# A trunk of S5 and gated delta layers on one core: the gated delta preparation at fixed steps, its decay and scores by whole units, its diagonal blocks inverted four chunks at a time

## The chip, the cores and the metric

The kernel runs on one core of one Trainium2 chip. The metric is device time in microseconds (us) of one execution, as the median of several runs. The core has five engines that work side by side and wait for each other through semaphores: TensorE (PE: matmuls into PSUM, its weight loads shown as PEld), VectorE (DVE), ScalarE (ACT), GpSimd (POOL) and SyncE (SP, which here only issues DMAs). Every engine works off its own program in order.

## The reference

Two layers are computed on 1,024 tokens of width 1,024. The first mixes tokens by an S5 scan; the second, where the change is, by a gated DeltaNet with 12 value heads and 6 key heads of width 128:

```python
q, k, v = jnp.split(silu(causal_conv(qkv, conv_w)), ...)     # q, k: 6 heads, l2-normed; v: 12 heads
g = -exp(a_log) * softplus(a + dt_bias);  beta = sigmoid(b)
# in chunks, with g summed up within a chunk:
decay = exp(where(causal, g[..., :, None] - g[..., None, :], -inf))
l_mat = where(strict, einsum('nbhid,nbhjd->nbhij', k * beta, k) * decay, 0.0)
t_mat = triangular_solve(l_mat, eye, left_side=True, lower=True, unit_diagonal=True)
u = t_mat @ v_beta;  w = t_mat @ (k_beta * exp(g))
intra = where(causal, (q @ k.T) * decay, 0.0)
# then a scan over the chunks with state, u, w, intra; rmsnorm; times silu(gate)
```

Each layer also attends to 256 memory tokens (4 heads), multiplies by a SiLU gate, and maps back to width 1,024.

## The kernel before, in words

The kernel uses chunks of 128 tokens, so there are 8 chunks; a chunk and a half of the heads (6 of 12) is a **unit** `(c, hf)`, 16 in all. What a chunk needs before the scan is the inverse of a unit lower triangular 128x128 matrix for each head.

**Projections.** A weight tile of 128 columns is loaded (`wraw`), split by ACT into a rounded half `whi` and by DVE into the rest `wlo`, and multiplied with the hidden state, split likewise into `hh` and `hl`. `mm3` (L110) issues three products, `pp<-hh,whi`, `pp<-hl,whi` and `pp<-hh,wlo`, for 8 slices of the width and 2 halves of the tokens: 48 matmuls of 128x512 for each tile. DVE then multiplies the two PSUM halves with the token norm (`scaled`, L260; into `cx` or `pj`). A tile is a *conv* tile (`conv`, L895: a multiplication and three multiply-adds of 128x1024 on DVE, a SiLU on ACT, then stored as `qkv`), an *attention input* or a *gate* tile (both only scaled, some with a SiLU, and stored).

**Up to the units.** `layer2` runs conv tiles 0 to 11 (q and k), turns each to token-major form by 8 transposes (`token_major`, L907: `ps_a<-ident,co`) and sums squares; `gdn_norms` (L923) makes the reciprocal norms `rq`, `rk` from them by a chain of small DVE operations, and `br` (beta times norm), which PE transposes (`ps_a<-ident,br`), ACT copies to `rows` and SP stores as `Brow`.

**A unit.** `load_kq` (L952) loads k and q; `g_scores` (L959) loads rows of G and of beta, broadcast, into `E` and `Eb`; 6 DVE operations form G_i - G_j and the causal mask (`E<-E,gG,negm`, L82), one ACT operation of 128x768 the exponential, POOL the product `Eb<-Eb,E` (L73); three matmuls `ps_a<-kq` (128x256) give k k' and k q', and 6 DVE operations multiply them out of PSUM with the norm and with `Eb` or `E` into `MT` and `AT`. The diagonal 32x32 blocks of `MT` go to DRAM (`Dm`), `AT` to `ATd`. `g_lower` (L985) transposes `MT` by 6 matmuls `ps_a<-ident,MT`; ACT copies what lies below the diagonal to `L`.

**The inverse.** `g_blocks` (L998) inverts the 32x32 diagonal blocks of one pair of chunks (96 blocks, one on each partition) by back substitution: 31 steps of two DVE operations, `XT<-XM,XN` and `XN<-XN,XT`, each over m*(32-m) elements. ACT transposes the result (`XM<-XN`), and SP stores both forms as `Dn` and `Dt`. `g_inverse` (L1017) loads the blocks of a unit (`N<-Dn`, `T<-Dt`) and builds the 128x128 inverse by four groups of small matmuls, y (`ps_a<-N,L`), z, y2 and z2, with ACT copies in between, and stores it as `Nd`.

**What sets the order.** `layer2` (L1257) runs a loop over p in 0 to 5: pair p's scores and lower parts, pair p-1's blocks, pair p-2's inverses, with three to five projection tiles (`fills`) between them. A scheduler then orders each engine's program by its own estimate of when operands are ready, so that PE takes other work where a unit's matmul isn't ready yet. Only where `self.pe.on` is set (in `before` around the S5 layer's groups) is PE kept in the order of the program: `Ordered.pin` (L44) asks for it.

After this stage come the scan steps with 8 more gate tiles, the attention, and the output projection; they are not changed.

Of the kernel before, what the change touches and what calls it, by code (L numbers as in the profile page):

```python
# [22 lines left out]
L = 1024  # L23
# [30 lines left out]
class Kern:  # L54
# [215 lines left out]
    def attention_inputs(self, h, wq, wg, rhs, wp):  # L270

        def one(w, dst, fn):
            t = self.tl(wp, (128, L), "pj")
            self.scaled(t, self.project([w], rhs), rhs[2], fn)
            self.dma(dst, t)

        return [partial(one, wq, self.qx[h], None), partial(one, wg, self.gx[h], AF.Silu)]
# [537 lines left out]
    def gdn_scalars(self, sp, wp, h):  # L815
# [68 lines left out]
        act.activation(eG, G, AF.Exp)  # L884
        self.rows(wp, G, self.Grow)
# [55 lines left out]
    def g_tiles(self, gp):  # L941
# [5 lines left out]
        self.Nb = [once(gp, (128, 6, 128), "N") for _ in range(2)]  # L947
        self.T64 = [once(gp, (64, 6, 64), "T64") for _ in range(2)]
# [10 lines left out]
    def g_scores(self, c, hf, gp):  # L959
        act, pe, tt, stt = self.act, self.pe, self.tt, self.stt  # L960
# [8 lines left out]
        act.activation(E, E, AF.Exp)  # L969
# [15 lines left out]
    def g_lower(self, MT, gp):  # L985
        act, pe = self.act, self.pe

        Lm = self.tl(gp, (128, 6, 96), "L", bufs=12)
# [9 lines left out]
    def g_blocks(self, pair, gp):  # L998

        n = 96  # L1000
        M, N = self.tl(gp, (n, 32, 32), "XM", bufs=1), self.tl(gp, (n, 32, 32), "XN", bufs=1)
        flat = "c b h j i -> (c b h) (j i)"
        self.dma(M.rearrange("p j i -> p (j i)"), self.Dm[pair].rearrange(flat))
        self.pool.memset(N, 0.0)
        self.v.memset(N.rearrange("p a b -> p (a b)")[:, 0:1024:33], 1.0)
        for m in range(31, 0, -1):
            w = 32 - m
            t = self.tl(gp, (n, 256), "XT", bufs=1)[:, 0:m * w].rearrange("p (j i) -> p j i", i=w)
# [4 lines left out]
        self.act.copy(T, N.rearrange("p j i -> p i j"))  # L1013
        for dst, src in ((self.Dn, N), (self.Dt, T)):
            self.dma(dst[pair].rearrange(flat), src.rearrange("p j i -> p (j i)"))

    def g_inverse(self, c, hf, gp, Lm):  # L1017

        act, pe = self.act, self.pe
        N, T64 = self.Nb[hf], self.T64[hf]  # L1020
# [8 lines left out]
        self.dma(T22[64:96], self.Dt[c // 2][c % 2, 2, h6].rearrange("h i j -> i h j"))  # L1029
        y = self.pa.tile([128, 6, 32], F32, name="ps_a", tag="ps_a")  # L1030
# [5 lines left out]
        for a in (0, 64):  # L1036
            act.copy(Y1[a:a + 32], y[a:a + 32])
        z = self.pa.tile([128, 6, 32], F32, name="ps_a", tag="ps_a")
# [9 lines left out]
        act.mul(T64[32:64, :, 0:32], z[32:64], -1.0)  # L1048
        y2 = self.pa.tile([128, 6, 64], F32, name="ps_a", tag="ps_a")
# [4 lines left out]
        act.copy(Y2, y2[0:64])  # L1054
        z2 = self.pa.tile([128, 6, 64], F32, name="ps_a", tag="ps_a")
# [201 lines left out]
    def layer2(self, st, h):  # L1257
# [7 lines left out]
        with P(name="cv", bufs=2, side="right") as wp:  # L1265
# [10 lines left out]
            with P(name="g1", bufs=2, side="right") as gp:  # L1276
                self.g_tiles(gp)
                units = [[(c, hf) for c in (2 * p, 2 * p + 1) for hf in range(2)] for p in range(4)]
                fills = [[partial(self.conv, ct, h, wp) for ct in range(12 + 3 * p, 15 + 3 * p)] for p in range(4)]
                fills += [[], []]  # L1280
                for hd in range(4):
                    fills[hd + 1] += self.attention_inputs(hd, A["g_w_in"][36 + hd], A["g_w_in"][40 + hd], h, wp)
                fills[4] += [partial(self.gate_tile, g, h, wp) for g in range(1)]
# [186 lines left out]
```

## Time and profile before

| what | us |
|---|---|
| median of 3 runs | 1955.84 (1953.41 to 1957.94) |
| the profiled execution's own time | 1961.59 |
| its span in the trace | 1959.9 |
| PE busy in the span | 1873.6 (96%) |
| DVE busy | 1316.7 (67%) |
| ACT busy | 941.2 (48%) |
| POOL busy | 170.9 (9%) |

The stage that the change rewrites lies between about 1118 and 1500 us of the span. The profile's page gives busy times, the chain of work that ended last, groups of instructions and DMA issues; beside it the trace can be asked for a table of windows (busy time of each engine, granted TensorE clock, DMA share), for the groups of one window, for what an engine waited for, and for a timeline of single instructions. A busy PE is not PE at its peak: a matmul's record reaches over the start of the next, so what a matmul costs is read from start to start.

### The profile page before, as it was taken

The numbers are of one execution on the slowest core, as the hardware profiler recorded it, in microseconds if no ns is written. First come the engines' busy times: TensorE is split into PE (matmuls) and PEld (weight loads), VectorE is DVE, ScalarE is ACT, GpSimd is POOL, SyncE is SP. The second block draws the span as 40 slices with busy tenths as digits, with TensorE's granted clock in tenths as the row PEclk, the third lists the DMA queues.
The fourth block names the chain that finished last, engine by engine and source line by source line (L and its number), as shares of the span: only waits on it lengthen the run. The fifth ranks groups of instructions, "written<-read, shape, count | busy, mean of one in ns | idle before, by whom it ended". The sixth has DMA issues, their size and how long they took to land.

```text
span 1959.9 us, 28842 instructions
## 1 busy us (share of the span) xinstructions
PE 1873.6 (96%) x10386; PEld 1528.9 (78%) x10386; DVE 1316.7 (67%) x2675; ACT 941.2 (48%) x1937; POOL 170.9 (9%) x100
## 2 busy tenths in 40 slices
PE   6899999999999998999999999899999999799897
PEld 6788888788878886888688877677777888588686
DVE  7888897895664423564566589869712787888744
ACT  5345688775554413443334444444334654555321
POOL 3100000000202131000000021110000000300400
PEclk9999999999999998999999999989999999999998
DMA  7445556554844434554223476656445765774752
GB/s 240 144 127 137 163 172 175 154 162 144 271 144 137 161 109 143 192 167 139 78 87 98 139 235 208 187 170 203 156 120 162 235 203 177 256 236 137 230 156 86
DMA packets 254446, 325.18 MB, mean 166 GB/s; under 512 B 80864, under 2 KB 176672, under 8 KB 254304
## 3 DMA queue, kind: packets, MB, share of 16 engines
q1 hardware_dynamic: 228960, 238.40, 39.4%
q10 hardware_dynamic: 25344, 84.95, 14.2%
q8 instruction: 82, 1.34, 0.3%
q14 instruction: 60, 0.49, 0.1%
HBM read 213.20 MB, written 93.95 MB: 157 GB/s over the span
## 4 chain that ended last, share of the span: by engine, by line
PE 77%; DVE 9%; DMA 6%; ACT 4%; issue 3%; SPq 1%; POOL 1%; ACTq 0%; DVEq 0%; POOLq 0%
PE pp L48 61%; PE ps_a L48 13%; PE ps_a L51 3%; DVE wlo L73 1%; DMA kq<-qkv 1%; SPq L70 1%; ACT whi L86 1%; DMA yr<-gy 1%; DMA zr<-oTd 1%; DVE co L82 1%; DVE E L82 1%; DVE XN L73 0%; DMA E<-Grow 0%; DVE ol L73 0%; DMA R<-E 0%
## 5 line engine op out<-in xcount | busy, mean ns | idle before, releaser
L48 PE MATMUL pp<-hh,whi 128*128 128x512 f32 x1216 | 493.4, 406 | 0.8 <-ACT hh L215 0.8
L48 PE MATMUL pp<-hl,whi 128*128 128x512 f32 x1216 | 481.9, 396 | 2.4 <-DVE hl L82 2.4
L48 PE MATMUL pp<-hh,wlo 128*128 128x512 f32 x1216 | 482.6, 397 | 0.0
L86 ACT CAST whi<-wraw 128x1024 fp32r<-128x1024 f32 (+1 forms) x180 | 183.7, 1021 | 410.5 <-PE pp L48 369.6
L73 DVE TENSOR_TENSOR wlo<-wraw,whi 128x1024 fp32r<-128x1024 f32 (+2 forms) x180 | 215.6, 1198 | 102.1 <-ACT whi L86 101.3
L48 PEld LDWEIGHTS pp<-hh,whi 128*128 128x128 f32 x1216 | 229.9, 189 | 50.8 <-issue 5.2
L48 PEld LDWEIGHTS pp<-hh,wlo 128*128 128x128 f32 x1216 | 229.7, 189 | 47.4
L48 PEld LDWEIGHTS pp<-hl,whi 128*128 128x128 f32 x1216 | 230.1, 189 | 46.0 <-DVE hl L82 3.3
L48 PE MATMUL pp<-oh,whi 128*128 128x512 f32 (+1 forms) x528 | 209.7, 397 | 9.9 <-ACT oh L86 6.8
L48 PE MATMUL pp<-oh,wlo 128*128 128x512 f32 (+1 forms) x528 | 207.8, 394 | 3.4 <-DVE wlo L73 3.3
L48 PE MATMUL pp<-ol,whi 128*128 128x512 f32 (+1 forms) x528 | 207.8, 394 | 1.5 <-DVE ol L73 1.5
L73 DVE TENSOR_TENSOR pj<-pp,hr 128x512 f32<-128x512 f32 x104 | 69.4, 687 | 115.6 <-PE pp L48 115.6
L48 PEld LDWEIGHTS pp<-oh,whi 128*128 128x128 f32 x528 | 100.5, 191 | 32.3 <-ACT oh L86 8.3
L48 PEld LDWEIGHTS pp<-oh,wlo 128*128 128x128 f32 x528 | 100.5, 190 | 26.8 <-DVE wlo L73 4.6
L48 PEld LDWEIGHTS pp<-ol,whi 128*128 128x128 f32 x528 | 100.4, 190 | 25.2 <-DVE ol L73 4.1
L48 PE MATMUL pp<-yl,whi 128*128 128x512 f32 x288 | 114.0, 396 | 0.5 <-DVE yl L73 0.5
L48 PE MATMUL pp<-yh,wlo 128*128 128x512 f32 x288 | 114.2, 396 | 0.0
L48 PE MATMUL pp<-yh,whi 128*128 128x512 f32 x288 | 113.7, 395 | 0.0
L82 DVE SCALAR_TENSOR_TENSOR co<-cx,conv_w,co 128x1024 f32<-128x1024 f32 x72 | 96.8, 1344 | 1.1
L73 POOL TENSOR_TENSOR ye<-yh,yl 128x1024 f32<-128x1024 f32 x12 | 29.7, 2478 | 617.8 <-DVE yl L73 443.0
L73 POOL TENSOR_TENSOR zr<-zr,zg 128x512 f32<-128x512 f32 x24 | 37.6, 1584 | 433.6 <-DMA kq<-qkv 296.2
L73 DVE TENSOR_TENSOR cx<-pp,hr 128x512 f32<-128x512 f32 x48 | 32.5, 688 | 58.5 <-PE pp L48 58.4
(350 smaller groups left out, 3258.0 us busy)
## 6 DMA issues: line engine op xcount, KB each, us to landing
wraw<-in_w_out_dram ACTq DMA_DIRECT2D x64, 512.0 KB, 4.0
wraw<-in_g_w_in_dram ACTq DMA_DIRECT2D x44, 512.0 KB, 4.3
wraw<-in_s_w_in_dram ACTq DMA_DIRECT2D x32, 512.0 KB, 4.0
R<-E SPq DMA_DIRECT2D x48, 256.0 KB, 3.8
gate<-pj SPq DMA_DIRECT2D x24, 512.0 KB, 3.9
qkv<-co SPq DMA_DIRECT2D x24, 512.0 KB, 2.8
kq<-qkv SPq DMA_DIRECT2D x60, 192.0 KB, 4.2
wraw<-in_w_glu_dram ACTq DMA_DIRECT2D x24, 384.0 KB, 3.6
```

The lines of the kernel that those rows point to most:

```text
L48: return self.pin(self.eng.matmul(*a, **kw))
L51: return self.pin(self.eng.transpose(*a, **kw))
L70: self.nc.sync.dma_start(out=out, in_=in_)
L73: (eng or self.v).tensor_tensor(out=out, in0=a, in1=b, op=op)
L82: self.v.scalar_tensor_tensor(out=out, in0=a, scalar=s, in1=b, op0=op0, op1=op1)
L86: self.act.copy(hi, src)
```

## The change

`layer2` hands the whole stage to a new function `g_units`, which puts everything at **steps**. A step is 6 of a tile's matmuls (one slice of the width), since projections are now generators that stop after each slice (`project_by_k`). Eight steps run ahead; from step 0 on, `self.pe.on` keeps PE in program order. The tiles follow each other as conv 12 to 18, the 8 attention inputs and 4 gates, conv 19 to 23. Unit u has its decay (loads, mask, exponential) prepared 6 steps ahead of its scores, the scores at step 6i for the first 8 units and 62+6i for the last 8, its lower part 4 steps after that. The blocks of chunks 0 to 3 begin at step 45, four of their 31 steps for every three steps of the tiles, those of chunks 4 to 7 at step 107. The inverse of unit u has its loads at s-4 and its y, z, y2 and z2 at s, s+3, s+6 and s+9, with s = 77+6i (first 8) or 139+5i (last 8).

The decay is now one masking addition of 128x768 on DVE, six exponentials of 128x128 on ACT with -G as bias (`nG`, a new small table), and `Eb*E` on DVE in place of POOL. The scores are copied out of PSUM by ACT, scaled by `rk`, over `kq`; then two DVE operations of 128x768 form `MT` in `Eb` and `AT` in `E`, so that the page will show `Eb` and `E` where it showed `MT` and `AT`. The blocks of four chunks are inverted together: the same 62 operations for a half of the sequence, each over twice the elements (`96x2x...`), and the memset, the transposing ACT copies and the stores twice for each. There are 4 `N` and 4 `T64` buffers in place of 2, 11 of `L` in place of 12, and 3 of the pool of projection tiles in place of 2, where the conv's output now shares the tag `pj`.

```diff
@@ conv
-        ps = self.project([self.A["g_w_in"][ct]], h)
-        x, o = self.tl(wp, (128, L + 3), "cx"), self.tl(wp, (128, L), "co")
+        ps = yield from self.project_by_k([self.A["g_w_in"][ct]], h)
+        x, o = self.tl(wp, (128, L + 3), "cx", bufs=2), self.tl(wp, (128, L), "pj")
@@ g_scores, now g_decay and g_scores
+        self.tt(E, E, self.negm.unsqueeze(1).broadcast_to([128, 6, 128]), ADD)
         for h in range(6):
-            stt(E[:, h], E[:, h], self.gG[:, c, 6 * hf + h:6 * hf + h + 1], self.negm, SUB, ADD)
-        act.activation(E, E, AF.Exp)
-        tt(Eb, Eb, E, MUL, self.pool)
-        AT, MT = self.tl(gp, sh, "AT"), self.tl(gp, sh, "MT")
-        for j in range(3):
-            ps = self.pa.tile([128, 2, 128], F32, name="ps_a", tag="ps_a")
-            pe.matmul(ps, lhsT=kq[:, j, 0], rhs=kq[:, j], start=True, stop=True)
-            rk = self.rk[:, c, 3 * hf + j:3 * hf + j + 1]
-            e2 = slice(2 * j, 2 * j + 2)
-            for i, (o, e) in enumerate(((MT, Eb), (AT, E))):
-                stt(o[:, e2], ps[:, i].unsqueeze(1).broadcast_to([128, 2, 128]), rk, e[:, e2], MUL, MUL)
+            q = 6 * hf + h
+            self.act.activation(E[:, h], E[:, h], AF.Exp, bias=self.gnG[:, c, q:q + 1])
+        self.tt(Eb, Eb, E, MUL)
+        return kq, E, Eb
+
+    def g_scores(self, c, hf, gp, kq, E, Eb):
+        for js in ((0, 1), (2,)):
+            ps = self.pa.tile([128, 2, 2, 128], F32, name="ps_a", tag="ps_a")
+            for j in js:
+                self.pe.matmul(ps[:, j % 2], lhsT=kq[:, j, 0], rhs=kq[:, j], start=True, stop=True)
+            for j in js:
+                q = 3 * hf + j
+                self.act.activation(kq[:, j], ps[:, j % 2], AF.Copy, scale=self.rk[:, c, q:q + 1])
+        MT, AT = Eb, E
+        for i, t in enumerate((MT, AT)):
+            t = t.rearrange("p (j e) i -> p j e i", e=2)
+            self.tt(t, kq[:, :, i].unsqueeze(2).broadcast_to([128, 3, 2, 128]), t, MUL)
@@ g_blocks
         for m in range(31, 0, -1):
             w = 32 - m
-            self.tt(t, M[:, 0:m, m:m + 1].broadcast_to([n, m, w]),
-                    N[:, m:m + 1, m:32].broadcast_to([n, m, w]), MUL)
-            self.tt(N[:, 0:m, m:32], N[:, 0:m, m:32], t, SUB)
-        T = self.tl(gp, (n, 32, 32), "XM", bufs=1)
-        self.act.copy(T, N.rearrange("p j i -> p i j"))
-        for dst, src in ((self.Dn, N), (self.Dt, T)):
-            self.dma(dst[pair].rearrange(flat), src.rearrange("p j i -> p (j i)"))
+            self.tt(t, M[:, :, 0:m, m:m + 1].broadcast_to([n, 2, m, w]),
+                    N[:, :, m:m + 1, m:32].broadcast_to([n, 2, m, w]), MUL)
+            self.tt(N[:, :, 0:m, m:32], N[:, :, 0:m, m:32], t, SUB)
+            yield
+        T = self.tl(gp, (n, 2, 32, 32), "XM", bufs=1)
+        for q in range(2):
+            self.act.copy(T[:, q], N[:, q].rearrange("p j i -> p i j"))
+            for dst, src in ((self.Dn, N), (self.Dt, T)):
+                self.dma(dst[2 * half + q].rearrange(flat), src[:, q].rearrange("p j i -> p (j i)"))
@@ g_units (new)
+        for u in range(16):
+            i, late = u % 8, u // 8
+            s = 6 * i + 62 * late
+            put(s - 6, prepare, u)
+            put(s, scores, u)
+            put(s + 4, lower, u)
+            s = (77 + 6 * i, 139 + 5 * i)[late]
+            put(s - 4, load, u)
+            for j in range(4):
+                put(s + 3 * j, inverse, u)
+        for half, s in ((0, 45), (1, 107)):
+            for i in range(32):
+                put(s + 3 * i // 4, blocks, ("b", half))
...
+        for t in range(-8, 0):
+            for what in at.pop(t, ()):
+                what()
+            next(go)
+        self.pe.on = True
+        for t in range(0, 1 + max(at)):
+            for what in at.pop(t, ()):
+                what()
+            next(go, None)
+        drain(go)
+        self.pe.on = False
```

The first place is PE where the stage begins. Before, 60 rows of `pp` stand between the last transposes of conv 11 (`ps_a<-ident_170,co`, 8 of them) and the transpose of `br`, and 25 more between that and the first scores (`ps_a<-kq`). These are the rows around `br` before:

```order
L48 MATMUL pp<-hh_7047,whi 128x512
L48 MATMUL pp<-hl_7048,whi 128x512
L48 MATMUL pp<-hh_7047,wlo 128x512
L51 MATMUL ps_a<-ident_170,br_9715 96x128
L48 MATMUL pp<-hh_7047,whi 128x512
L48 MATMUL pp<-hl_7048,whi 128x512
L48 MATMUL pp<-hh_7047,wlo 128x512
```

And the rows around it now, of which the first ones are the end of what stands behind those transposes (`ps_a<-ident_170,pj` now), 12 rows of `pp` in all:

```order
L48 MATMUL pp<-hh_7047,wlo 128x512
L48 MATMUL pp<-hh_7047,whi 128x512
L48 MATMUL pp<-hl_7048,whi 128x512
L48 MATMUL pp<-hh_7047,wlo 128x512
L51 MATMUL ps_a<-ident_170,br_9717 96x128
L48 MATMUL ps_a<-kq 128x256 x3
L48 MATMUL pp<-hh_7047,whi 128x512
L48 MATMUL pp<-hl_7048,whi 128x512
```

The scores of unit 0 now stand right behind `br`, and `br` 12 matmuls behind the last transposes in place of 60.

The second place is DVE in the middle of a block inversion; `XT` and `XN` are its two operations in turn. Before (the first pair's, with the mask operations of a unit and a conv tile's multiply-adds between them):

```order
L82 SCALAR_TENSOR_TENSOR co<-cx,conv_w_182,co 128x1024
L73 TENSOR_TENSOR XT<-XM,XN 96x207
L82 SCALAR_TENSOR_TENSOR E<-E,gG_8514,negm_9730 128x128
L73 TENSOR_TENSOR XN<-XN,XT 96x23x9
L82 SCALAR_TENSOR_TENSOR E<-E,gG_8514,negm_9730 128x128
L73 TENSOR_TENSOR XT<-XM,XN 96x220
L82 SCALAR_TENSOR_TENSOR E<-E,gG_8514,negm_9730 128x128
L73 TENSOR_TENSOR XN<-XN,XT 96x22x10
L82 SCALAR_TENSOR_TENSOR E<-E,gG_8514,negm_9730 128x128
L73 TENSOR_TENSOR XT<-XM,XN 96x231
```

And now (the first half's, with the score products `Eb<-kq,Eb` and `E<-kq,E` of unit 8 and an attention input's scaling and weight split between them):

```order
L73 TENSOR_TENSOR XT<-XM,XN 96x462
L73 TENSOR_TENSOR Eb<-kq,Eb 128x768
L73 TENSOR_TENSOR XN<-XN,XT 96x2x21x11
L73 TENSOR_TENSOR E<-kq,E 128x768
L73 TENSOR_TENSOR XT<-XM,XN 96x480
L73 TENSOR_TENSOR pj<-pp,hr_7049 128x512 x2
L73 TENSOR_TENSOR wlo<-wraw,whi 128x1024
L73 TENSOR_TENSOR XN<-XN,XT 96x2x20x12
L73 TENSOR_TENSOR XT<-XM,XN 96x494
L73 TENSOR_TENSOR XN<-XN,XT 96x2x19x13
```

Each operation of the inversion has twice the elements, and there are half as many of them in all; six small mask operations for each unit have given way to whole-unit ones.

The third place is PE where the first inverse begins (`ps_a<-N,L` is y of unit 0). Before:

```order
L48 MATMUL pp<-hl_7048,whi 128x512
L48 MATMUL pp<-hh_7047,wlo 128x512
L48 MATMUL ps_a<-N_9735,L 32x32
L48 MATMUL pp<-hh_7047,whi 128x512
L48 MATMUL pp<-hl_7048,whi 128x512
L48 MATMUL pp<-hh_7047,wlo 128x512
L48 MATMUL pp<-hh_7047,whi 128x512
L48 MATMUL pp<-hl_7048,whi 128x512
L48 MATMUL ps_a<-N_9735,L 32x32 x11
L48 MATMUL pp<-hh_7047,wlo 128x512
```

And now:

```order
L48 MATMUL pp<-hl_7048,whi 128x512
L48 MATMUL pp<-hh_7047,wlo 128x512
L48 MATMUL ps_a<-N_9737,L 32x32 x12
L48 MATMUL pp<-hh_7047,whi 128x512
L48 MATMUL pp<-hl_7048,whi 128x512
L48 MATMUL pp<-hh_7047,wlo 128x512
L48 MATMUL pp<-hh_7047,whi 128x512
L48 MATMUL pp<-hl_7048,whi 128x512
L48 MATMUL pp<-hh_7047,wlo 128x512
```

Before, the scheduler put the 12 matmuls of y apart, with `pp` rows among them; now they stand together at their step, 77, and every later `pp` row stands behind them.

More of the change, by code (lines that the diff above doesn't have):

```diff
@@ L272, in one @@
         def one(w, dst, fn):
+            ps = yield from self.project_by_k([w], rhs)
             t = self.tl(wp, (128, L), "pj")
-            self.scaled(t, self.project([w], rhs), rhs[2], fn)
+            self.scaled(t, ps, rhs[2], fn)
             self.dma(dst, t)
-        return [partial(one, wq, self.qx[h], None), partial(one, wg, self.gx[h], AF.Silu)]
+        return [one(wq, self.qx[h], None), one(wg, self.gx[h], AF.Silu)]
     def attention(self, layer, h, half, ap, dst):
@@ L884, in gdn_scalars @@
         act.activation(eG, G, AF.Exp)
+        act.mul(P("nG"), G, -1.0)
         self.rows(wp, G, self.Grow)
@@ L946, in g_tiles @@
                                 fill=-1e30, base=0, channel_multiplier=-1)
-        self.Nb = [once(gp, (128, 6, 128), "N") for _ in range(2)]
-        self.T64 = [once(gp, (64, 6, 64), "T64") for _ in range(2)]
+        self.Nb = [once(gp, (128, 6, 128), "N") for _ in range(4)]
+        self.T64 = [once(gp, (64, 6, 64), "T64") for _ in range(4)]
         for t in self.Nb + self.T64:
@@ L1054, in g_inverse @@
         act.copy(Y2, y2[0:64])
+        yield
         z2 = self.pa.tile([128, 6, 64], F32, name="ps_a", tag="ps_a")
@@ L1059, in g_inverse, with g_units, prepare, scores @@
         self.dma(self.Nd[c, hf], N)
+    def g_units(self, h, wp, gp):
+        A = self.A
+        units = [(c, hf) for c in range(8) for hf in range(2)]
+        decay, mt, low, inv = {}, {}, {}, {}
+        def prepare(u):
+            decay[u] = self.g_decay(*units[u], gp)
+        def scores(u):
+            mt[u] = self.g_scores(*units[u], gp, *decay.pop(u))
+        def lower(u):
+            low[u] = self.g_lower(mt.pop(u), gp)
+        def blocks(i):
+            if i not in inv:
+                inv[i] = self.g_blocks(i[1], gp)
+            next(inv[i], None)
+        def load(u):
+            inv[u] = self.g_inverse(*units[u], gp, low.pop(u))
+            next(inv[u])
+        def inverse(u):
+            next(inv[u], None)
+        at = {}
+        def put(t, what, arg):
+            at.setdefault(t, []).append(partial(what, arg))
+        for u in range(16):
[11 more added lines that the diff above has]
+                put(s + 3 * i // 4, blocks, ("b", half))
+        light = [one for hd in range(4) for one in
+                 self.attention_inputs(hd, A["g_w_in"][36 + hd], A["g_w_in"][40 + hd], h, wp)]
+        light += [self.gate_by_k(g, h, wp) for g in range(4)]
+        tiles = [self.conv_by_k(ct, h, wp) for ct in range(12, 19)] + light
+        tiles += [self.conv_by_k(ct, h, wp) for ct in range(19, 24)]
+        def steps():
+            for one in tiles:
+                yield from one
+        go = steps()
+        for t in range(-8, 0):
[9 more added lines that the diff above has]
+        self.pe.on = False
@@ L1264, in layer2 @@
             self.gdn_scalars(sp, wp, h)
-        with P(name="cv", bufs=2, side="right") as wp:
+        with P(name="cv", bufs=3, side="right") as wp:
             with P(name="tm", bufs=2, side="right") as tp:
@@ L1277, in layer2 @@
                 self.g_tiles(gp)
[L1278 to L1283, printed above, removed]
-                fills[5] += [partial(self.gate_tile, g, h, wp) for g in range(1, 4)]
-                Lm = {}
-                for p in range(6):
-                    mt, lag = [], []
-                    fill = iter(fills[p])
-                    if 0 < p < 5:
-                        self.g_blocks(p - 1, gp)
-                    for i in range(5):
-                        if i < 4 and p < 4:
-                            mt.append((units[p][i], self.g_scores(*units[p][i], gp)))
-                        if i and p < 4:
-                            u, m = mt.pop(0)
-                            Lm[u] = self.g_lower(m, gp)
-                        next(fill, lambda: None)()
-                        if i < 4 and p >= 2:
-                            u = units[p - 2][i]
-                            self.g_inverse(*u, gp, Lm.pop(u))
+                self.g_units(h, wp, gp)
         g2 = ExitStack()
```

29 lines of the change are left out of this document (19 added, 10 removed).

## The prediction

> **What bounds the kernel now.** I read the table of windows over the stage that is rewritten first, to see whether PE is short of work there, then the groups of instructions of that stretch, then the timelines. Columns of the table: window and length, then busy us (instructions) of PE, PEld, DVE, ACT and POOL, the granted TensorE clock, DMA share, GB/s.
>
> ```profile
> 1160.00:1200.00 40.00, 36.41 (x165) 28.37 (x164) 35.06 (x72) 17.23 (x26) 9.56 (x4) 1.00 0.75 226
> 1200.00:1240.00 40.00, 38.30 (x176) 30.74 (x175) 38.63 (x95) 20.27 (x27) 7.14 (x3) 1.00 0.67 205
> 1240.00:1280.00 40.00, 36.80 (x279) 27.52 (x278) 35.53 (x82) 17.30 (x27) 5.60 (x2) 0.87 0.56 162
> 1280.00:1320.00 40.00, 37.65 (x288) 28.47 (x287) 24.01 (x61) 19.75 (x36) 6.43 (x4) 0.87 0.65 201
> ```
>
> PE is the bound, but DVE is close behind it: 35 to 39 of 40 us up to 1280. PE idles 3.6 + 1.7 + 3.2 + 2.4 = 10.9 us in these four windows, and in the last two the granted clock is 0.87, worth 2 x 40 x 0.13 = 10.4 us. So there are some 21 us here that a smoother order could win, and not more: the matmuls themselves are the same before and after.
>
> The groups of the stretch from 1111 to 1490 us (busy us, mean ns of one | idle before):
>
> ```profile
> L82 DVE SCALAR_TENSOR_TENSOR co<-cx,conv_w,co 128x1024 f32<-128x1024 f32 x39 | 54.4, 1395 | 0.3
> L73 DVE TENSOR_TENSOR XN<-XN,XT 96x31 f32<-96x31 f32 (+15 forms) x124 | 47.1, 380 | 2.0
> L73 DVE TENSOR_TENSOR XT<-XM,XN 96x31 f32<-96x31 f32 (+15 forms) x124 | 41.7, 336 | 8.8 <-DMA XM<-Dm 6.9
> L73 POOL TENSOR_TENSOR Eb<-Eb,E 128x768 f32<-128x768 f32 x16 | 35.7, 2232 | 187.0 <-ACT E L969 169.6 <-DMA N<-Dn 17.4
> L82 DVE SCALAR_TENSOR_TENSOR E<-E,gG,negm 128x128 f32<-128x128 f32 x96 | 32.2, 359 | 2.3 <-DMA E<-Grow 2.3
> L73 DVE TENSOR_TENSOR wlo<-wraw,whi 128x1024 fp32r<-128x1024 f32 x25 | 30.5, 1222 | 1.5 <-ACT whi L86 1.3
> ...
> L48 PE MATMUL ps_a<-Y,T 32*32 32x32 f32 (+1 forms) x506 | 25.1, 210 | 1.1 <-ACT Y L1037 1.1
> L82 DVE SCALAR_TENSOR_TENSOR MT<-ps_a,rk,Eb 128x256 f32<-128x256 f32 x48 | 22.8, 475 | 10.6 <-POOL Eb L73 10.5
> ...
> L73 DVE TENSOR_TENSOR pj<-pp,hr 128x512 f32<-128x512 f32 x24 | 16.4, 691 | 70.5 <-PE pp L48 70.5
> ```
>
> **The change part by part.** *Whole-unit decay and scores.* A unit's mask and score operations cost DVE 6 x 0.359 + 3 x 0.475 + as much for AT = 5.0 us. Now there are four operations of 128x768 (mask, Eb, MT, AT). No row has that size; between the 0.69 of 512 elements and the 1.22 of 1024 it is about 0.96 each, 3.8 a unit, although Eb comes over from POOL (2.23 there). DVE wins 1.2 x 16 = 19 us. ACT gets five more exponentials and three copies a unit; it is half idle here (17 to 20 of 40 us), so I cost that at nothing beyond its place in the chain of a unit.
>
> *Double-width blocks.* These rows are from a pair's inversion that ran alone on DVE:
>
> ```profile
> 1389.71 0.20 DVE L73 TENSOR_TENSOR XT<-XM,XN 96x31 f32<-96x31 f32 x1 [4.37 <-DMA XM<-Dm]
> 1389.95 0.21 DVE L73 TENSOR_TENSOR XN<-XN,XT 96x31 f32<-96x31 f32 x1
> ...
> 1404.24 0.42 DVE L73 TENSOR_TENSOR XT<-XM,XN 96x256 f32<-96x256 f32 x1
> 1404.69 0.42 DVE L73 TENSOR_TENSOR XN<-XN,XT 96x256 f32<-96x256 f32 x1
> ```
>
> From start to start 0.24 us at 31 elements and 0.45 at 256: 0.21 us and 0.96 ns an element. The 31 steps of m(32-m) elements sum to 5,456, so a pair takes 62 x 0.21 + 2 x 5,456 x 0.96 ns = 23.5 us and a double one 13.0 + 21.0 = 34.0. Four pairs took 94, two halves take 68. DVE wins 26 us more in sum; but each half now comes as one run of 34, and what it is wanted for stands at a fixed place on PE.
>
> *The start.* What PE, DVE and SP do there now:
>
> ```profile
> 1118.40 0.77 PE L51 MATMUL ps_a<-ident,co 128*128 128x128 f32 x5
> ...
> 1133.36 0.31 PE L51 MATMUL ps_a<-ident,br 128*96 128x128 f32 x1 [0.26 <-DVE br L73]
> ...
> 1139.00 0.40 PE L48 MATMUL pp<-hh,whi 128*128 128x512 f32 x1
> 1139.24 1.02 PE L48 MATMUL ps_a<-kq 128*128 128x256 f32 x4
> ```
>
> ```profile
> 1124.24 0.20 DVE L77 TENSOR_SCALAR nv<-ssq 128x96 f32<-128x96 f32 x1
> ...
> 1131.32 0.26 DVE L82 SCALAR_TENSOR_TENSOR qke<-qkt,qke 128x96 f32<-128x96 f32 x1
> 1131.61 0.26 DVE L73 TENSOR_TENSOR qkt<-qke 128x96 f32<-128x96 f32 x1
> ```
>
> ```profile
> 1134.00 0.33 SPq L70 DMA_DIRECT2D Brow<-rows  x1
> 1134.39 0.95 SPq L70 DMA_DIRECT2D kq<-qkv  x2
> ```
>
> A pp matmul is 0.23 us from start to start. The 60 of them after the last transposes covered 13.8 us, which the DVE chain from nv to br needed. Now 12 stand there: PE is done at 1119.4 + 2.8 = 1122.2. The chain begins at 1124.24 at the earliest; its 17 operations, free of the conv tile's between them, take 0.29 each: br at 1129.2. PE idles 7.0 us. Then come the scores of unit 0: in the trace SP issued Brow 0.64 us after br's transpose, and the kq loads behind it end their issue at 1135.34; with a landing of some 3 us the scores can begin about 4 us after br (3 to 5.9, the trace's own distance from 1133.36 to 1139.24). Then 24 pp (5.5 us) until the transposes of MT_0, which need rows of E and Eb loaded through the same queue, six exponentials and three DVE operations:
>
> ```profile
> E<-Grow SPq DMA_DIRECT2D x16, 384.0 KB, 5.1
> ...
> Dm<-MT SPq DMA_DIRECT2D x64, 24.0 KB, 2.3
> XM<-Dm SPq DMA_DIRECT2D x4, 384.0 KB, 4.1
> ...
> N<-Dn SPq DMA_DIRECT2D x64, 24.0 KB, 2.2
> ```
>
> E is issued about 2 us after br, lands 5.1 later, and mask, exponentials (6 x 0.3), Eb and MT follow: br + 12, when PE is there at br + 10.5, and DVE has the mask of unit 1 queued ahead: I take 5, from 2 to 6. Start: 7 + 4 + 5 = 16 us (9 to 19).
>
> *Units 0 to 7.* PE needs 36 pp (8.3), the scores (1.0) and transposes (0.8): 10.1 us a unit. DVE needs three quarters of a conv tile (4 x 1.395 at most, 2 x 0.69 and 1.22 for wlo: 6.1) and 3.8: 9.9 at most. No wait, by a thin margin: 0 to 3 us, taken as 0.
>
> *Half 0's blocks.* The M load waits for MT_7 (scores at step 42): copies, MT, the Dm stores (four issues and 2.3), the load's 4.1: some 13 us, so it lands near step 51. From there PE has 26 steps of 1.4 us, three scores and three lower parts: 41 us to y of unit 0 at step 77. On DVE's program between the first XT and the last XN of this half stand, beside the 34.0 us of the blocks, 14 whole-unit operations of units 8 to 12 (13.4), scaling and weight split of three attention inputs (3 x 2.6) and two multiply-adds (2.8): 58 us. Behind that comes the tail that one sees here, a pair's (chain of waits):
>
> ```profile
> 1240.98 2.15 ACT XM L1013
> 1243.14 5.11 DMA Dt<-XM
> ```
>
> The transposing copies are now two (4.3), and SP stands with its program behind the second one, since both halves' Dn and Dt are issued ahead of the first N load; then four issues (1.9) and 2.2: 9 us. 58 + 9 - 41 = 26 us in which PE stands at y with every later pp behind it. Dependent operations hide some of their fixed time when others stand between them, and M can land a step or two earlier, so I take 21 (10 to 32). Before, PE took other pp there.
>
> *Half 1's blocks.* M lands near step 114, 25 steps (35 us) ahead of step 139; three inverses lie between (25.1 / 14 = 1.8 us each for the Y,T kind alone, some 3.5 in all): 46. DVE: 34 and four light tiles, 44, and the tail: 53. That is 7; I take 4 (0 to 15), since this half has little else on DVE.
>
> *The clock.* In the windows from 1240 the clock fell although no idle time of PE in them was long, and 10.4 us went. After three or four real idles I count one stretch of half clock each, 7 us in sum (3 to 12). The Trainium skill, "TensorE: Matmul & The Clock Gate", Part 1, has it that an idle window of about 3.4 us halves the clock until about 3.4 us of sustained work: an estimate from it is 1.7 us for each of four idles, 7 us, but by it the falls in the rows above should not have come at all; the rows decide, and they allow more.
>
> *What goes.* PE's waits of before in this stage (10.9) and its clock falls (10.4): -21 us if all go, and I let all go (-12 if half of the waits only move).
>
> **Sum.** 16 + 21 + 4 + 7 - 21 = +27 us on the profiled execution's 1961.6: 1988.6. The median of the runs is 5.8 below that execution, so I forecast 1983 us. Behind 1500 us nothing changes: conv 23's output stands behind the last inverses as far as I see, beside gate tiles.
>
> **The rivals.** *A, the blocks keep up (faster).* Place: y of unit 0. The run of half 0 must end within 41 - 9 = 32 us of the M load, not 58, for PE not to wait; that needs most of the other 24 us done ahead of the load, while DVE has nothing else to do. It is the point that decides. For it: DVE was under 39 of 40 us busy and now has 19 + 26 = 45 us less to do over the stage, and it may idle ahead of the load. Against it: the order has those operations between the block operations, and an engine keeps its order. With no wait at half 1 either, 3 at half 0 and 4 for the clock, the sum is the start (9 to 16) + 3 + 0 + 4 - 21 = -5 to +2 on the median, 1951 to 1958, and lower by 3 to 6 where the small matmuls, no longer strewn among pp, cost PE less: value 1951, range 1945 to 1958.
>
> *B, a draw.* Half 0 waits 8 us, the start costs 13, the clock 4: 1955.8 + 8 + 13 + 4 + 0 - 21 = 1960, a few us either way.
>
> *C, worse.* A two-level pattern (`96x2x20x12`) pays its fixed part twice: 62 x 0.21 = 13 us more on DVE in each half, which PE pays in full at both: 1983 + 26 = 2009. No row shows such a pattern.
>
> *D, the order is not held.* If PE's program were not the one printed, the waits would be filled as before and DVE's relief alone would tell: 1956 less some half of the 21 us, 1945. The printed rows speak against it.
>
> **Chances.** Forecast 0.56, A 0.24, B 0.06, C 0.08, D 0.06. The forecast's own range takes its bounds (start 9 to 19, half 0 10 to 32, half 1 0 to 15, clock 3 to 12), not all at one end: 1962 to 2003. The range reaches down to the lower end of A: 1945 to 2003. A measurement here tells about 0.2% (4 us) from no change. Faster: three quarters of A, D, little of B, 0.25; same: the rest of A and some of B, 0.08; slower: the forecast, C and the rest, 0.67.
>
> **What would show it.** In the profile of the changed kernel: PE idle of 7 us ahead of br's transpose and about 4 ahead of the first scores; one wait of PE of 10 to 30 us at the first `ps_a<-N,L`, released by a load of N, while DVE is busy without a gap from the first XT to the last XN; a small one at unit 8's; granted clock under 1 right after each. XT and XN groups of 62 with means near 0.5 us. Wrong: no wait over 5 us at the first y, or a DVE that has gaps between block operations; or a start without idle.

## The result, and the profile after

The changed kernel takes 1977.91 us (median of 4 runs, 1974.73 to 1980.69), the kernel before 1956.4 in the runs beside it: a ratio of 1.0111, with a 95% interval of 1.0091 to 1.0131. The change makes it 21.5 us slower; 27 were forecast. The profiled execution of the changed kernel took 1974.73 us, 3.2 below its median, where that of before was above its own; so the two traces are compared stage by stage and not by their ends. They differ ahead of the stage too: the last transposes of conv 11 begin at 1118.40 us in the trace before and at 1113.12 in the one after, though nothing there was changed. One of the eight runs of experiment 12 below took 2618.88 us at a granted clock of 0.65 and is left out of that kernel's median.

The table of windows of the changed kernel (columns as before):

```profile
1160.00:1200.00 40.00, 39.49 (x184) 32.58 (x182) 32.29 (x37) 30.02 (x61) 0.00 (x0) 1.00 0.85 255
1200.00:1240.00 40.00, 37.65 (x173) 31.41 (x174) 35.90 (x53) 21.45 (x42) 0.00 (x0) 1.00 0.56 181
1240.00:1280.00 40.00, 20.98 (x99) 17.19 (x97) 34.13 (x56) 19.61 (x39) 0.00 (x0) 0.82 0.60 182
1280.00:1320.00 40.00, 34.90 (x349) 28.28 (x350) 11.15 (x15) 19.71 (x47) 1.81 (x1) 0.88 0.64 177
```

The third row is the result in one line: PE is busy for 21 of 40 us while DVE works for 34. Afterwards DVE has little to do (11 of 40). DVE's load over the stage did fall; it is bunched where PE can't go on without it.

What PE waited for in the stage (1105 to 1530 us): sum, times, longest.

```profile
PE ps_a L48 <- DMA N<-Dn: 29.7, 3, 24.1
PE ps_a L51 <- DVE br L73: 5.3, 1, 5.3
PE ps_a L48 <- DMA kq<-qkv: 5.0, 1, 5.0
PE ps_a L51 <- DVE Eb L73: 3.9, 2, 2.9
```

That is 43.9 us. The same list of the kernel before (1111 to 1490 us) sums to 13.2 us over eight kinds, of which these are the largest three and the one on N:

```profile
PE ps_a L51 <- DVE MT L82: 2.9, 2, 1.7
PE ps_a L48 <- DVE AT L82: 2.5, 4, 0.8
PE ps_a L48 <- ACT T L1048: 2.3, 1, 2.3
PE ps_a L48 <- DMA N<-Dn: 1.9, 1, 1.9
```

So 30.7 us of waits came on. From the last transposes of conv 11 to the first transposes of v in the next stage, the kernel before takes 1509.76 - 1118.40 = 391.4 us and the changed one 1524.94 - 1113.12 = 411.8, 20.4 more; PE's other time there fell by some 10 us (what of, stands in the table under *What goes* below).

The start and the end of the stage on PE, and between them the first y (timelines of after):

```profile
1113.12 1.09 PE L51 MATMUL ps_a<-ident,pj 128*128 128x128 f32 x8
...
1122.30 0.45 PE L51 MATMUL ps_a<-ident,br 128*96 128x128 f32 x1 [5.32 <-DVE br L73]
1127.79 2.90 PE L48 MATMUL ps_a<-kq 128*128 128x256 f32 x6 [5.04 <-DMA kq<-qkv]
1138.12 0.88 PE L51 MATMUL ps_a<-ident,Eb 128*128 128x128 f32 x6 [1.09 <-DVE Eb L73]
...
1260.60 0.39 PE L48 MATMUL pp<-hh,wlo 128*128 128x512 f32 x1
1285.10 0.59 PE L48 MATMUL ps_a<-N,L 32*32 32x32 f32 x6 [24.12 <-DMA N<-Dn]
...
1524.94 0.85 PE L51 MATMUL ps_a<-ident,vT 128*128 128x128 f32 x6 [0.40 <-DMA vT<-qkv]
```

And what PE waited for at that y: the last operation of the block inversion on DVE, then the tail on ACT, SP and the queue. The first operation of the run stands ahead of it.

```profile
1221.25 0.26 DVE L73 TENSOR_TENSOR XT<-XM,XN 96x62 f32<-96x62 f32 x1
...
1276.33 0.22 DVE L73 TENSOR_TENSOR XN<-XN,XT 96x62 f32<-96x62 f32 x1
1276.61 0.34 SPq L70 DMA_DIRECT2D Dn<-XN  x1
1276.63 3.75 ACT L1031 COPY XM<-XN 96x1024 f32<-96x1024 f32 x2 [2.21 <-DVE XN L73]
1278.59 0.33 SPq L70 DMA_DIRECT2D Dt<-XM  x1
1278.96 0.42 SPq L70 DMA_DIRECT2D Dn<-XN  x1
1280.41 0.30 SPq L70 DMA_DIRECT2D Dt<-XM  x1
1280.77 3.13 SPq L70 DMA_DIRECT2D N<-Dn  x4
```

The run takes 1276.55 - 1221.25 = 55.3 us (with one gap of 1.4, for a load of E), the tail 8.5 more; PE has 39.7 us of work in that time and waits for the rest. The first load of N is issued only behind both pairs of stores. "Released by a DMA" in the list of waits is thus the end of a chain that is nearly all DVE. The durations that the sum was made with also show in the groups:

```profile
L73 DVE TENSOR_TENSOR XT<-XM,XN 96x62 f32<-96x62 f32 (+15 forms) x62 | 32.4, 522 | 8.9 <-DMA XM<-Dm 7.2
L73 DVE TENSOR_TENSOR XN<-XN,XT 96x62 f32<-96x62 f32 (+15 forms) x62 | 32.3, 522 | 1.6
...
L73 DVE TENSOR_TENSOR E<-E,negm 128x768 f32<-128x768 f32 x16 | 15.3, 956 | 33.2 <-DMA E<-Grow 31.1 <-DMA N<-Dn 2.1
L73 DVE TENSOR_TENSOR Eb<-Eb,E 128x768 f32<-128x768 f32 x16 | 15.2, 952 | 10.0 <-DMA N<-Dn 8.0 <-ACT E L975 1.9
```

A whole-unit operation takes 0.95 to 0.96 us (0.96 was taken), and the 124 operations of the inversion 64.7 us busy in place of 88.8 for 248.

### The profile page after: what moved, and what is told of

It reads as the page before. It is cut to its first block, busy times and chain, and to the rows that moved or that the text cites. A ratio compares the mean times of both kernels' runs of the same rounds, so it can differ in the third digit from the quotient of the medians.

```text
span 1973.0 us, 28704 instructions
## 1 busy us (share of the span) xinstructions
PE 1860.1 (94%) x10386; PEld 1528.3 (77%) x10386; DVE 1287.5 (65%) x2423; ACT 973.0 (49%) x2064; POOL 135.0 (7%) x86
## 5 line engine op out<-in xcount | busy, mean ns | idle before, releaser
L86 ACT CAST whi<-wraw 128x1024 fp32r<-128x1024 f32 (+1 forms) x180 | 183.6, 1020 | 360.8 <-PE pp L48 342.8
L48 PE MATMUL pp<-oh,whi 128*128 128x512 f32 (+1 forms) x528 | 208.8, 396 | 11.1 <-ACT oh L86 6.8
L82 DVE SCALAR_TENSOR_TENSOR pj<-cx,conv_w,pj 128x1024 f32<-128x1024 f32 x72 | 92.3, 1283 | 1.6
L73 POOL TENSOR_TENSOR ye<-yh,yl 128x1024 f32<-128x1024 f32 x12 | 29.7, 2479 | 613.8 <-DVE yl L73 437.5
```

Of the source, the lines that this page charges most:

```text
L48: return self.pin(self.eng.matmul(*a, **kw))
L73: (eng or self.v).tensor_tensor(out=out, in0=a, in1=b, op=op)
L82: self.v.scalar_tensor_tensor(out=out, in0=a, scalar=s, in1=b, op0=op0, op1=op1)
L86: self.act.copy(hi, src)
```

## The experiments

Twelve kernels were run, in three groups, each beside runs of the kernel before on its chip (medians 1955.1, 1956.1 and 1956.5 us); ratios are to those.

**1. The start left to the scheduler.** If the idle time ahead of `br` and of the first scores is a term of its own, filling it wins that much.

```diff
-        for t in range(-8, 0):
+        for t in range(-8, 14):
...
-        for t in range(0, 1 + max(at)):
+        for t in range(14, 1 + max(at)):
```

> The changed kernel with the first 14 steps of the units also left to the scheduler (PE is kept in order from step 14 on, not from step 0), so that projection matmuls can stand ahead of the transpose of br and of the first scores. My theory: the 10.4 us of PE idle ahead of br and the first scores, the 1.3 us at the first MT and the 2 us of half clock behind them go, the wait of 24 us at the first y stays: 1978 - 13 = 1965 us (1961 to 1969). Rival, the waits only move: units start as late as before, DVE is the bound up to step 77, and the wait at the first y grows by what the start saves: 1976 to 1980 us, with a first wait at y of 30 us or more.

Measured: 1982.01 us, ratio 1.0141 (1.0123 to 1.016). The rival was right that nothing is won, though not in how. PE's two large waits in this kernel:

```profile
PE ps_a L48 <- DMA N<-Dn: 28.5, 3, 23.0
PE ps_a L51 <- DVE Eb L73: 13.5, 4, 5.3
```

The 10.4 us ahead of `br` and the scores are gone. The conv tile's operations, back among the small ones of the chain, now bring `br` 15.0 us behind the last transposes (1132.51 against 1117.53) in place of 9.2, the first units come as much later, and their transposes wait 13.5 us in place of 3.9. The wait at the first y, 23.0 us, is nearly what it was (24.1), and didn't grow as the rival had it. In the whole stage PE idles 42.4 us in place of 44.4, and half clock costs about 6 us more (13.5 against 7.5, as counted in the table under *What goes*): the idle time moved, and the clock took more than the rest.

**2. PE left to the scheduler throughout.**

```diff
-        self.pe.on = True
         for t in range(0, 1 + max(at)):
```

> The changed kernel with PE left to the scheduler throughout (the same operations, steps and buffers; only the request to keep PE in program order is gone). My theory: the kept order is what turns DVE's block run into a PE wait; unpinned, other projections fill it, DVE's relief of 45 us shows, and the time is below the kernel before: 1938 to 1954 us, with no PE wait over 5 us in the stage. Rival, the steps themselves (unit work too late on DVE) set the end: the waits stay within 8 us of the changed kernel's, 1968 to 1978 us.

Measured: 1944.32 us, ratio 0.9948 (0.9931 to 0.9965): 33.6 us faster than the change and faster than the kernel before. The largest of the waits that are left, and the windows that showed the result:

```profile
PE ps_a L51 <- DVE Eb L73: 8.5, 5, 2.2
```

```profile
1240.00:1280.00 40.00, 38.02 (x172) 31.31 (x171) 38.24 (x60) 15.01 (x32) 0.00 (x0) 1.00 0.56 175
1280.00:1320.00 40.00, 40.00 (x383) 31.52 (x382) 14.07 (x23) 23.94 (x46) 1.81 (x1) 1.00 0.62 165
```

DVE is as bunched as in the changed kernel (38 and 14 us), but PE is busy beside it, and its clock doesn't fall. The kept order is what turned DVE's run into a wait of PE.

**3. The blocks by pairs, in the kept order.**

```diff
-        for half, s in ((0, 45), (1, 107)):
+        for pair, s in ((0, 45), (1, 61), (2, 107), (3, 123)):
             for i in range(32):
-                put(s + 3 * i // 4, blocks, ("b", half))
+                put(s + i // 2, blocks, ("b", pair))
```

and `g_blocks` of single width for one pair, as before, but with two buffers each of XM and XN in place of one.

> The changed kernel with its blocks inverted pair by pair as before (62 operations of single width for each pair, four pairs), the pairs at steps 45, 61, 107 and 123; all else as changed, PE kept in order. DVE has 26 us more to do. My theory: the first y needs only pair 0, which is inverted by about step 65, so the wait of 24 us at it goes, as does the one of 5 us at the first late inverse, and the half clock behind both (4 us): 1978 - 33 = 1945 us (1940 to 1953). Rival, DVE's total is the bound: 26 us more on DVE come out as more PE waits at the later units' scores or inverses: 1978 to 2000 us.

Measured: 1955.29 us, ratio 1.0006 (0.999 to 1.0022). 22.6 us faster than the change although DVE has more to do; the rival falls, and my number was too low by 10. The waits on N fell from 29.7 us to those below; those at the start stayed, and some 3 us came on at the scores and as much at the transposes. Together PE's idle time in the stage fell from 44.4 to 23.1 us and the cost of half clock from 7.5 to 5.2, which is the gain.

```profile
PE ps_a L48 <- DMA kq<-qkv: 8.0, 2, 4.4
PE ps_a L51 <- DVE Eb L73: 6.6, 3, 3.6
PE ps_a L51 <- DVE br L73: 5.3, 1, 5.3
PE ps_a L48 <- DMA N<-Dn: 2.5, 2, 1.3
```

**4. The product Eb*E back on POOL.**

```diff
-        self.tt(Eb, Eb, E, MUL)
+        self.tt(Eb, Eb, E, MUL, self.pool)
```

> The changed kernel with the product Eb*E back on POOL as before. Between the first XT and the last XN of half 0 DVE loses four such products, 0.95 us each as its trace shows. My theory: the wait at the first y is the end of DVE's run, so it falls by about 4 us, from 24 to 20 us. Rival, the wait is set by the DMA queue and the loads behind the run: it stays at 24 us. Third: POOL's 2.2 us and its share of memory ports put later MTs off, and lower parts wait: 3 us or more of new waits at transposes.

Measured: 1982.16 us in one run; the wait at the first y is 26.7 us, not 20, and waits at transposes are 9.7 in place of 3.9. Neither of the first two expectations holds: the wait at the first y grew. The third does, with 5.8 us of new waits at transposes. One run tells little of the total, so the trace is read instead. DVE's run takes 57.7 us, 2.4 more, although the four products no longer stand in it. These rows say why (timeline, POOL and DVE):

```profile
1236.96 3.05 POOL L73 TENSOR_TENSOR Eb<-Eb,E 128x768 f32<-128x768 f32 x1 [9.42 <-ACT E L975]
...
1238.23 2.16 DVE L73 TENSOR_TENSOR XT<-XM,XN 96x350 f32<-96x350 f32 x1
1240.43 0.52 DVE L73 TENSOR_TENSOR XN<-XN,XT 96x350 f32<-96x350 f32 x1
```

The same 350 elements take 2.16 us beside POOL's product and 0.52 without it. In the run, XT and XN have means of 629 and 574 ns where the changed kernel has 522 and 521: 5.0 us more over 62 operations, for 3.8 us of products taken off; one more multiply-add (1.28) stands in the run too, and the three sum to 2.5. So the run does set the wait, but POOL's products cost DVE more there than its own.

**5. All that is behind the first units, 8 steps later.**

```diff
-            s = 6 * i + 62 * late
+            s = 6 * i + 70 * late
...
-            s = (77 + 6 * i, 139 + 5 * i)[late]
+            s = (85 + 6 * i, 147 + 5 * i)[late]
...
-        for half, s in ((0, 45), (1, 107)):
+        for half, s in ((0, 45), (1, 115)):
```

> The changed kernel with everything behind the first 8 units 8 steps later: scores of the late units at 70+6i, first inverses at 85+6i, blocks of half 1 from step 115, late inverses at 147+5i; half 0's blocks stay at step 45. PE has 8 steps (11 us) more to do ahead of the first y, DVE one attention input (2.5 us) more in its run. My theory: the wait at the first y falls from 24 to about 15 us and the rest stays, 1978 - 9 = 1969 us. Rival, the end takes it back: the last inverses now end at step 191 of 192, with nothing behind them to cover the last conv tile's chain, so the time stays at 1975 to 1981 us although the wait at the first y falls.

Measured: 1972.9 us, ratio 1.0078 (1.0053 to 1.0103), 5 us faster than the change. The longest wait on N fell from 24.1 to 12.2 us, about the 11 us of projections that now stand ahead of it; DVE's run is no longer for it (54.3 us, 1227.08 to 1281.36). The total gained less than half of that. The end, which the rival spoke of, isn't where it went: PE waits 0.6 us at the first transposes of v, where it waited 0.4. The stage's idle time on PE fell by 10.7 us (44.4 to 33.8), but half clock costs about 3 us more (10.7 against 7.5); what is left of the difference isn't accounted for.

**6. PE left to the scheduler, blocks by pairs** (experiments 2 and 3 together).

> The changed kernel with PE left to the scheduler and the blocks inverted pair by pair (steps 45, 61, 107, 123). DVE has 26 us more to do than with double width and PE unpinned (1944 us). My theory: with PE free to take other work DVE's total isn't the bound, so double width is worth little in itself: 1941 to 1949 us. Rival, DVE's relief is where the unpinned kernel's gain comes from: 1952 us or more, about the kernel before.

Measured: 1949.35 us, ratio 0.9973 (0.995 to 0.9997). Between the two expectations; against experiment 2 (0.9931 to 0.9965) the intervals overlap. By the medians double width is worth some 5 us where PE is free, and that isn't shown clear of noise.

**7. Only the whole-unit decay and scores, in the kernel before.**

```diff
-                            mt.append((units[p][i], self.g_scores(*units[p][i], gp)))
+                            mt.append((units[p][i], self.g_scores(*units[p][i], gp, *self.g_decay(*units[p][i], gp))))
```

with `g_decay`, `g_scores` and `nG` of the changed kernel.

> The kernel before with only the decay and the scores by whole units (its loop over pairs, its blocks, its buffers and its unpinned PE as before). DVE has 19 us less to do. My theory: in the first windows of the stage DVE is 35 to 39 of 40 us busy and PE waits for MT and AT there, so some of it shows: 1946 to 1952 us against 1955. Rival, off the path: 1953 to 1957 us, and then the unpinned gain comes from the steps or from the blocks. Third, Eb on DVE in place of POOL delays MT: over 1957 us.

Measured: 1947.34 us, ratio 0.9952 (0.9931 to 0.9973). As my theory had it. Part of the gain is no operation that went: groups that the edit doesn't touch became shorter. The multiply-adds of the conv tiles had a mean of 1,395 ns before and XN one of 380; now:

```profile
L82 DVE SCALAR_TENSOR_TENSOR co<-cx,conv_w,co 128x1024 f32<-128x1024 f32 x37 | 47.1, 1274 | 0.2
L73 DVE TENSOR_TENSOR XN<-XN,XT 96x31 f32<-96x31 f32 (+15 forms) x124 | 41.6, 336 | 2.7
```

That is 0.12 us for each multiply-add and 5.5 us over the 124 XN (XT had 336 ns in both). It fits the effect of experiment 4: in the trace before, the multiply-add that starts at 1258.94 us, beside POOL's product of 1256.43 to 1260.70, takes 2.84 us, and the one just ahead of it 1.27.

**8. PE in the kept order from step 92 on only.**

```diff
-        self.pe.on = True
         for t in range(0, 1 + max(at)):
+            self.pe.on = t >= 92
```

> The changed kernel with PE kept in order only from step 92 on (scores and lower parts of the first 13 units and the first inverses are the scheduler's to place). My theory: the cost of the kept order lies where DVE is behind, ahead of and at the first y; what is left is the 5 us at the first late inverse and its half clock: 1946 to 1953 us. Rival, the kept order costs everywhere alike (about 30 us over 190 steps): half of it would stay, 1958 to 1965 us.

Measured: 1976.25 us, ratio 1.0103 (1.0074 to 1.0132). Both expectations fall. The first y still waits:

```profile
PE ps_a L48 <- DMA N<-Dn: 23.4, 2, 16.3
PE ps_a L51 <- DVE Eb L73: 7.2, 5, 2.3
```

By the order asked for, projections from step 92 on can't pass z2 of unit 1 and z of unit 2, which need the same half's blocks, so only the 15 steps between are there to fill. PE did use them: it stopped at 1278.3 us, where the changed kernel stopped at 1261.0, and then stood until N came. What follows is the work of the units that had piled up, with no projection in it until 1321.34, and the clock stayed low through it:

```profile
1292.00:1322.00 30.00, 25.43 (x265) 19.91 (x266) 5.06 (x8) 13.00 (x37) 1.81 (x1) 0.50 0.50 129
```

```profile
1294.58 0.28 PE L48 MATMUL ps_a<-N,L 32*32 32x32 f32 x2 [16.26 <-DMA N<-Dn]
...
1321.34 0.99 PE L48 MATMUL pp<-hh,whi 128*128 128x512 f32 x1
```

25 us busy at half clock there are about 12 us lost (an estimate: half of the busy time), more than the wait had become shorter.

**9. Blocks by pairs and the start left to the scheduler** (experiments 1 and 3 together).

> The kernel of the pairs (blocks pair by pair, PE kept in order), with the first 14 steps of the units left to the scheduler as in the first experiment. There is no long wait at the first y in which a saving at the start could be lost. Theory A, the start's idle of 12 us is a term of its own that the wait at the first y merely hid in the first experiment: 1955 - 10 = 1945 us (1941 to 1949). Theory B, filling the start puts the first units later and their transposes wait instead (13 us of such waits in the first experiment), whatever comes behind: 1952 to 1960 us.

Measured: 1956.79 us, ratio 0.9999 (0.9982 to 1.0016), against 1.0006 for the pairs alone. Theory B: the waits at transposes are 13.4 us in place of 6.6, those at the first scores and `br` go, and nothing is won. PE's idle time in the stage falls by 2.9 us (23.1 to 20.2), not by the 9.7 that stood at `br` and the first scores, and half clock costs about 4 more (9.1 against 5.2).

**10. Half of the inversion's steps left out.**

```diff
-        for m in range(31, 0, -1):
+        for m in range(31, 15, -1):
```

> The changed kernel with 15 of the 31 steps of each block inversion left out (those for m from 15 down to 1), so that its output isn't the reference's. DVE's run has 30 operations of 5,200 elements in sum less: 30 x 0.21 + 5.0 + 5.0 = 16 us in each half. My theory: the end of DVE's run sets the first y, so the wait there falls from 24 to about 8 us, the one at the first late inverse goes, and the time falls by 16 + 5 and some half clock: 1978 - 23 = 1955 us. Rival, the loads and the queue behind the run: waits of 18 us or more stay, 1972 us or more.

Measured: 1956.35 us, ratio 1.0002 (0.9988 to 1.0017), 21.6 us faster than the change. PE's waits:

```profile
PE ps_a L48 <- DMA N<-Dn: 6.6, 3, 3.3
PE ps_a L51 <- DVE br L73: 5.3, 1, 5.3
PE ps_a L51 <- DVE Eb L73: 4.7, 2, 2.9
PE ps_a L48 <- DMA kq<-qkv: 4.6, 2, 4.3
```

The run of half 0 is 28.9 us (1227.51 to 1256.46): with fewer steps, fewer other operations lie among them too. What is left at the first y, 3.3 us, is no longer DVE's: SP issues the loads of N only at 1264.17, 7.7 us behind the end of the run. With the start, the order, the queue, the stores and loads all as in the changed kernel, shorter DVE runs take the waits on N from 29.7 to 6.6 us, and the time back to that of the kernel before. The cause of the slowdown is the length of those runs ahead of a fixed place on PE.

**11 and 12. Three buffers of E and Eb**, in experiment 7 and in experiment 6 (there with one buffer of XM and XN).

```diff
-        E, Eb = self.tl(gp, sh, "E"), self.tl(gp, sh, "Eb")
+        E, Eb = self.tl(gp, sh, "E", bufs=3), self.tl(gp, sh, "Eb", bufs=3)
```

> The kernel before with only the decay and the scores by whole units (1947 us), and three buffers of E and Eb in place of two, so that a unit's loads and its mask can run further ahead. If loads of E behind the store of AT hold up units, 1942 to 1946 us; if not, 1945 to 1949 us.

> The changed kernel with PE left to the scheduler, blocks pair by pair (one buffer of XM and XN), and three buffers of E and Eb. PE waited 11 us at the transposes of MT in the unpinned kernel of the pairs (1949 us). If that comes from loads of E and Eb that wait for a buffer: 6 us or more of it goes, 1940 to 1944 us; if from DVE's order, 1947 to 1951 us.

Measured: 1944.11 us, ratio 0.9934 (0.9911 to 0.9957), and 1944.18 us, ratio 0.9947 (0.9927 to 0.9968). The first lies in the range given for its first case, but its interval overlaps with that of experiment 7 (0.9931 to 0.9973); the second lies by a hair beyond its first case, and its interval overlaps with that of experiment 6. So what the third buffer is worth stays open. In the second the waits at transposes did fall from 11.1 to 2.6 us, and 6.1 us on N came in their place. With experiments 2 and 7 these are the fastest kernels of the study, each about 0.5 to 0.7% below the kernel before; their intervals overlap.

## Why the prediction was right, point by point

*The direction and the cause* were right: one long wait at the first y, released by a load of N, with DVE at work throughout. Worked out, taken and measured:

| step of the prediction | taken, us | measured, us |
|---|---|---|
| half 0: DVE's run | 58 | 55.3 |
| tail behind it | 9 | 8.5 |
| PE's work ahead of the first y | 41 | 39.7 |
| wait at the first y | 21 (26 worked out) | 24.1 |
| wait at the first late inverse | 4 | 5.0 |
| idle ahead of br | 7 | 5.3 |
| ahead of the first scores | 4 | 5.0 |
| ahead of the first MT | 5 | 1.1 |
| units 0 to 7 | 0 (0 to 3) | 2.9 |

*Half 0.* Right in its working, and experiments 2, 3, 5 and 10 agree: each takes the wait away or shortens it from a different side. The allowance of 5 us that I took off the worked-out 26 was not needed in full.

*The start* was sized 4.6 us too large (16 against 11.4): the chain of small operations began 3.9 us behind the start of the last transposes, where 5.8 had been read from before, and the first MT came early enough. As idle time of PE it does stand in the sum. What the prediction didn't see is that it isn't a loss that can be filled by itself: in experiments 1 and 9 the waits at `br` and the first scores go, and the idle time of the stage falls by only 2.0 and 2.9 us. `br` comes early because nothing else is on DVE; if PE's gap is filled with projections, DVE's chain and the units behind it come later, and their transposes wait instead.

*The clock.* 7 us were taken. Half clock while PE worked lasted about 4.5 us behind the first scores, 4.3 behind the first y and 6.4 behind the first late inverse, by windows of 1 us; these are wider ones of the changed kernel:

```profile
1128.00:1132.00 4.00, 4.00 (x10) 3.14 (x11) 1.08 (x3) 0.66 (x3) 0.31 (x1) 0.50 0.95 318
1132.00:1136.00 4.00, 4.00 (x18) 3.21 (x18) 3.75 (x5) 3.63 (x10) 0.00 (x0) 0.96 0.25 95
1285.00:1289.00 4.00, 3.90 (x31) 3.04 (x32) 0.14 (x2) 0.62 (x2) 0.25 (x1) 0.50 0.33 51
1412.00:1416.00 4.00, 2.80 (x28) 2.34 (x29) 0.00 (x0) 0.62 (x2) 0.00 (x0) 0.53 0.38 137
1416.00:1420.00 4.00, 4.00 (x12) 3.10 (x12) 0.00 (x0) 0.00 (x0) 0.00 (x0) 0.62 0.34 55
```

Half of their 15 us is 7.5 us lost, an estimate. The loss of 10.4 us before that was to go is 10.2 by the same count. The rule quoted from the Trainium skill ("TensorE: Matmul & The Clock Gate", Part 1), some 3.4 us of work at half clock after a long idle, comes near the first two; the third took longer.

*What goes.* 21 us were taken. 30.7 us of waits came on net, where 16 + 21 + 4 - 11 = 30 were forecast; that these agree so well is in part luck, since the start came out 4.6 us smaller and the two waits at inverses and that of the units (0 taken) 7 us larger, while before 13.2 us of waits stood where 10.9 had been taken. The rest can be split by windows of 1 us over the stage, from the last transposes of conv 11 to the first of v. "Half clock" is PE's busy time times what the granted clock lacks of 1, an estimate of what the clock cost:

| kernel | stage, us | PE idle | half clock | the rest |
|---|---|---|---|---|
| before | 391.4 | 13.2 | 10.2 | 367.9 |
| changed | 411.8 | 44.4 | 7.5 | 359.9 |
| 1, start left to the scheduler | 415.3 | 42.4 | 13.5 | 359.4 |
| 2, order not kept | 377.0 | 8.9 | 0.0 | 368.2 |
| 3, pairs | 389.2 | 23.1 | 5.2 | 360.8 |
| 7, whole units only, order not kept | 378.3 | 8.5 | 2.7 | 367.1 |
| 8, order kept from step 92 | 410.4 | 33.1 | 17.9 | 359.4 |
| 9, pairs and start | 389.5 | 20.2 | 9.1 | 360.2 |
| 10, half of the steps | 388.0 | 21.4 | 6.8 | 359.9 |

So the clock gave 2.7 us net (10.4 - 7 = 3.4 were forecast), and 8 us came from a term that the forecast had at nothing: what PE needs for the matmuls themselves, waits and clock apart. It goes with the kept order: 359 to 361 us in the kernels that keep it (355.7 in experiment 5, where 16 projection matmuls fewer stand in the stage), 364 to 368 in the others. Rival A had named 3 to 6 us for small matmuls that stand together. This term is most of the difference between 27 forecast and 20.4 measured in the stage. Its cause stays open: PE changes between projections and other matmuls 245 times in the stage before and 155 times now, and loses about 0.1 us at a change (0.32 or 0.34 us to the next start in place of 0.23), but experiment 2 has 151 changes and saves nothing.

*The rivals.* A asked for most of the other operations to run ahead of the M load; the run held them as the order had them. Experiments 3 and 10 reached 1955 and 1956 us, between the values of A and B, by other edits. C falls: the mean of XT, 522 ns at a mean of 352 elements, is what 0.96 ns an element and one fixed part make, less the gap between starts. D falls with the long wait, and experiment 2 shows its value: 1944 us for an unkept order, where 1945 was given.

## What to carry to other kernels

A kept order on the bounding engine makes every late operand into idle time, so ahead of each fixed place add up what the slower engine's own program has between the operand's first input and its last step, all that is interleaved included, and hold it against the work ahead of that place. A saving in the slower engine's total says nothing if its work is bunched into one run that a place must wait for; halves that finish early (a pair, here) beat fewer and wider operations as long as that order is kept. And an idle time can be won back only if what follows it doesn't wait for something that the same idle time lets happen sooner: fill it in an experiment before counting on it.

## What the runs showed of the hardware that was not expected

A POOL product of two SBUF tensors holds up DVE operations beside it: 2.16 us for an XT that takes 0.52 otherwise (experiment 4), and with the products gone from POOL the multiply-adds of the conv tiles went from 1,395 to 1,274 ns and XN from 380 to 336 (experiment 7). So moving Eb to DVE cost 0.95 us each, 15 us for 16, and gave some 10 of that back in these two groups alone; the prediction counted only the cost. In experiment 4 three operations of the run took 2.16 to 2.29 us, and each ended 0.4 to 0.5 us behind POOL's product. The Trainium skill, "SBUF — State Buffer", section "SBUF: two separate sides", has it that DVE and GpSimd share a pair of ports as an exclusive lock, where the loser blocks for the whole instruction; the 2.16 us and those ends agree.

The granted clock can stay at half while PE is busy: 0.50 over 1292 to 1322 us in experiment 8, with PE at 25.4 of 30 us, where the changed kernel came back to full clock some 4 us after a longer wait. What held it there wasn't tried; from 1294.58 to 1321.34 us only matmuls of units and inverses ran, most of them of 32 or 64 rows, and full clock came back at 1322.9, soon after the projections. And the stretches of half clock come in steps: by windows of 1 us they last 13.6 and 6.8 us in the kernel before, 10.2, 23.9 and 6.8 in the changed one and 40.9 in experiment 8, which are 4, 2, 3, 7, 2 and 12 times 3.41 us. If that holds beyond these traces, what a wait costs in clock depends on where it falls; no run was made for it.
